# A hybrid encoder's attention and delta-rule scan in a fixed order of TensorE batches

## The chip, the cores and the metric

One core of a Trainium2 chip runs the whole program in one launch. The metric is the device time in microseconds (us), the median of several runs. One further execution was profiled; the rows below are from it.

## What is computed

Two layers on 512 tokens of width 1024, all in float32. Each layer is a feed-forward block (gate, up, down), a mixer and a second feed-forward block, each behind a root-mean-square norm and added to the stream. The mixer projects the stream to 16 heads of three kinds: 4 dense attention heads, 6 attention heads with a mask and a bias by distance, and 6 heads of a gated delta rule that is run over the tokens forwards and backwards. Their outputs go through one output projection.

The attention heads and the delta rule, cut to what matters here:

```python
s = q @ k.T * D ** -0.5 (+ bias);  p = softmax(s);  o = p @ v
...
T = triangular_solve(eye + M, eye)          # per chunk of 64 tokens, lower, unit diagonal
u, w = T @ vb, T @ (kb * exp(gc))
def step(state, xs):                        # 8 chunks, one behind the other
    v_new = u_i - w_i @ state
    o = (q_i * exp(g_i)) @ state + a_i @ v_new
    state = state * exp(g_last) + (k_i * exp(g_last - g_i)).T @ v_new
    return state, o
```

## The kernel before

Weights stream in by DMA and are split into two parts of 32 bits (`whi`, `wlo`), activations too (`xh`, `xl`), so that three matmuls stand for one in float32; the feed-forward blocks are made of these alone. In the mixer `project_c`, `project_z` and `project_groups` make the heads' inputs (`pc`, `pgr`), `delta_solve` inverts the chunks' triangular blocks, and `attention` runs the attention heads and, between them, the scan.

`delta_solve` inverts 32x32 diagonal blocks on VectorE (forward direction, d = 0) and GpSimd (d = 1), passes them through DRAM, and joins two blocks into one of 64 by two rows of 32x32 products (L649 into `pp1`, L658 into `pp2`), direction by direction and block by block: 12 products of one block, then 12 of the next. ScalarE copies `pp1` to `p1s` (L653) and `pp2` into `Y` (L662), 32 rows at a time.

`attention` has five tiles of two heads, and four query blocks (t) of 128 tokens each: 20 units. `scores` issues four matmuls into two `psc` (L868, L869), takes the row maximum on VectorE (L876, or L880 with the bias) and the exponential on ScalarE (L877, L882), and divides by the sum on GpSimd (L884). `weigh` transposes the probabilities on TensorE into `ppt` (L894), ScalarE copies them to `pth` (L896), and 8 matmuls of two halves add the values into `pav` (L900). `load(i)` transposes queries and keys into `pqk` (L813) and makes the split operands `qs`, `kh` on ScalarE (L820, L832) and `qs`, `kl` on VectorE (L821, L833); it is called at t = 2 of the tile ahead. `ppt` and `pqk` share two PSUM buffers, `psc` has two.

`delta_scan` is a generator with one step per chunk, which serves both directions (d) at once: products with the state `S` into `pkq` (L685), the right-hand side on VectorE (L688, L689, L691), the product with the inverse into `prr` (L697), `vn` (L700), the state's update into `pS` (L707, with GpSimd at L713 and VectorE at L715), and the output into `po` (L720, L727, L729, L731). Every matmul of float32 operands except a transpose is two records in a trace. `delta_finish` norms the output, transposes it into `pot` (L946) and multiplies by the gate; `project_out` is `pwo`.

A scheduler of the language sets each engine's order before the program runs, by priorities and an estimate of times. The order in which the code issues the work is only its starting point: it may put a unit's two transposes apart and other batches between them. `AHEAD = 1` puts `weigh` one unit behind `scores`, and `SCAN_AT` issues one whole scan step at every second unit:

```python
        for tile_ in range(5):
            for t in range(NT):
                pending.append(scores(tile_, t))
                if len(pending) > AHEAD:
                    weigh(*pending.pop(0))
                unit = 4 * tile_ + t
                for _ in range(SCAN_AT.count(unit)):
                    next(scan)
```

Of the kernel before, what the change touches and what calls it, by code (L numbers as in the profile page):

```python
# [29 lines left out]
SCAN_AT = (0, 2, 4, 6, 8, 10, 12, 14)  # L30
FINISH_AT = 15
LOAD_AT = 2
# [80 lines left out]
class Body:  # L113
# [205 lines left out]
    def mixer(self, n, l, sm, nxt):  # L319
# [4 lines left out]
        with scope("mix") as mp:  # L324
# [6 lines left out]
            with scope("qkv") as qkvp:  # L331
# [3 lines left out]
                with scope("scan") as sp, scope("scanp", space=PSUM) as m.ps:  # L335
# [10 lines left out]
                    with scope("outp", space=PSUM, **right) as pp:  # L346
                        if FINISH_AT >= 20:
                            m.delta_finish(sp)
                        m.project_out(pp, qkvp, nxt)


class Mixer:
# [244 lines left out]
    def delta_solve(self, pool):  # L597
# [42 lines left out]
        for d in range(2):  # L640
            y = self.Y[d]
            lo_a, lo_b = (0, 32) if d == 0 else (32, 0)
            rows = [(slice(64 * hf + lo_a, 64 * hf + lo_a + 32), slice(64 * hf + lo_b, 64 * hf + lo_b + 32)) for hf in range(2)]
            for tp in range(2):
                p1 = self.aux("pp1")
                for ra, rb in rows:
                    for q in range(12):
                        t, h = 2 * tp + q // 6, q % 6
                        nc.tensor.matmul(out=p1[rb, q * 32:q * 32 + 32], lhsT=y[ra, t, h, lo_b:lo_b + 32],  # L649
                                         rhs=X[ra, t * 6 + h], start=True, stop=True)  # L650
                ps = pool.tile([P, 384], F32, name="p1s")
                for ra, rb in rows:
                    nc.scalar.activation(out=ps[rb], in_=p1[rb, 0:384], func=AF.Copy)  # L653
                p2 = self.aux("pp2")
                for ra, rb in rows:
                    for q in range(12):
                        t, h = 2 * tp + q // 6, q % 6
                        nc.tensor.matmul(out=p2[ra, q * 32:q * 32 + 32], lhsT=ps[rb, q * 32:q * 32 + 32],  # L658
                                         rhs=y[rb, t, h, lo_b:lo_b + 32], start=True, stop=True)
                for ra, rb in rows:  # L660
                    dst = y[ra, 2 * tp:2 * tp + 2].rearrange("p t h i -> p (t h) i")[:, :, lo_b:lo_b + 32]
                    nc.scalar.activation(out=dst, in_=p2[ra, 0:384].rearrange("p (q i) -> p q i", i=32), func=AF.Copy)  # L662

    def delta_scan(self, sp):
# [8 lines left out]
        for s in range(8):  # L673
# [6 lines left out]
            if s > 0:  # L680
                pkq = two("pkq")
                for i in range(2):
                    for d, ch, t, r in dirs:
                        for pr in range(3):
                            nc.tensor.matmul(out=pkq[r, i, pr * P:pr * P + P], lhsT=self.kq[pr][:, i, ch], rhs=S[:, d, pr],  # L685
                                             start=True, stop=True)
# [5 lines left out]
            else:  # L692
                rhs = self.vs[:, 0]
            pr_ = self.aux("prr")
            for h in range(6):
                for d, ch, t, r in dirs:
                    nc.tensor.matmul(out=pr_[r, h * 64:h * 64 + 64], lhsT=self.Y[d][r, t, h],  # L697
                                     rhs=rhs[r, h * 64:h * 64 + 64], start=True, stop=True)
            vn = sp.tile([P, 384], F32, name="vn")
            nc.vector.tensor_tensor(out=hd(vn), in0=hd(pr_[:, 0:384]),  # L700
                                    in1=self.step[:, 0, s].unsqueeze(2).to_broadcast(sh), op=ALU.mult)
            if s < 7:
                pS = two("pS")
                for d, ch, t, r in dirs:
                    for h in range(6):
                        pr, par = divmod(h, 2)
                        nc.tensor.matmul(out=pS[64 * par:64 * par + 64, d, pr * 64:pr * 64 + 64],  # L707
                                         lhsT=self.kd[d][r, t, h * 64:h * 64 + 64], rhs=vn[r, h * 64:h * 64 + 64],
                                         start=True, stop=True)
# [8 lines left out]
            for h in range(6):  # L718
                for d, ch, t, r in dirs:
                    nc.tensor.matmul(out=po[r, h * 64:h * 64 + 64], lhsT=self.A[d][r, t, h],  # L720
                                     rhs=vn[r, h * 64:h * 64 + 64], start=True, stop=True)
# [75 lines left out]
    def attention(self, ap, pp, scan, sp):  # L797
# [3 lines left out]
        low, high = slice(0, 64), slice(64, 128)  # L801
        kept, pads = [], [ap.tile([P, 2, T], F32R, name=f"kl{i}") for i in range(2)]
# [7 lines left out]
        def turned(qkv, tl):  # L810
            p = pp.tile([P, T], F32, name="pqk", tag="t", bufs=2)
            for t in range(NT):
                nc.tensor.transpose(out=p[:, t * P:t * P + P], in_=qkv[:, t, tl * P:tl * P + P], identity=ident)  # L813
# [23 lines left out]
        ops = {}  # L837

        def load(i):
            if i < 2:  # L840
                if i == 0:
                    kv = keys(turned(self.qkv[0], 2), 1.0), self.qkv[0][:, :, 384:512]
                else:
                    kv = ops[0][1:]
                ops[i] = (queries(turned(self.qkv[0], i), 0.125), *kv)
            elif i < 5:
                g = self.qkv[i - 1]
                ops[i] = (queries(turned(g, 0), self.gq8), keys(turned(g, 1), self.nbk), g[:, :, 256:384])
# [3 lines left out]
        def scores(tile_, t):  # L852
            if t == 0:
                state["pv"] = pp.tile([P, T], F32, name="pav", tag="v")
# [7 lines left out]
            if t == LOAD_AT:  # L862
                load(tile_ + 1)
# [57 lines left out]
        for u in pending:  # L921
            weigh(*u)
# [136 lines left out]
```

## Time and profile before

| | us |
|---|---|
| median of 3 runs | 2238.77 |
| lowest, highest | 2235.66, 2243.84 |
| the profiled execution's time | 2234.65 |
| its span, first to last instruction | 2232.6 |
| TensorE busy in the span | 2179.1 (98%) |
| VectorE, ScalarE, GpSimd busy | 1138.8, 789.5, 483.7 |

The time of the profiled execution is its span and 2 us around it. Busy time of TensorE is the union of its records, whose ends are modelled: matmuls are pipelined, and a record is longer than the distance to the next. In a timeline, a row merges records of one line that follow each other; in square brackets stand the idle time before it and what ended that.

### The profile page before, as it was taken

How to read it: one execution, taken by the hardware profiler on the slowest of the kernel's cores; microseconds unless marked ns; L12 is line 12 of the kernel's file. 1: busy time of each engine (PE TensorE's matmuls, PEld its weight loads, DVE VectorE, ACT ScalarE, POOL GpSimd, SP SyncE). 2: the span in 40 equal slices, each digit the busy share in tenths (PEclk: the TensorE clock that was granted, in tenths of full speed). 3: DMA queues.
4: the chain of work that ended last, by engine and by line, in shares of the span. 5: the costliest groups of instructions: out<-in, count | busy, mean ns of one | idle time of the engine just before them, and what ended most of it. 6: DMA issues, size and time to landing. Idle time of an engine off the chain costs nothing.

```text
span 2232.6 us, 30294 instructions
## 1 busy us (share of the span) xinstructions
PE 2179.1 (98%) x12212; PEld 1745.9 (78%) x12212; DVE 1138.8 (51%) x1881; ACT 789.5 (35%) x1153; POOL 483.7 (22%) x490
## 2 busy tenths in 40 slices
PE   7999999998999999999999999999989999999999
PEld 5888887778777888888788888877787778888887
DVE  5333334688677533333443333347795765333333
ACT  4222223524565322222332222235345643222221
POOL 3101012217253210101121010123073531101010
PEclk9999999999999999999999999999999999999999
DMA  5433333232302333333233333332331033333333
GB/s 172 127 95 94 96 95 120 81 82 85 92 18 95 95 94 95 95 90 98 86 95 94 95 91 98 92 126 67 100 103 47 28 105 92 94 93 93 96 92 102
DMA packets 93076, 206.82 MB, mean 93 GB/s; under 512 B 38561, under 2 KB 39073, under 8 KB 92936
## 3 DMA queue, kind: packets, MB, share of 16 engines
q1 hardware_dynamic: 91168, 199.98, 30.0%
q10 hardware_dynamic: 1768, 4.91, 0.8%
q8 instruction: 96, 1.57, 0.3%
q14 instruction: 44, 0.36, 0.1%
HBM read 193.83 MB, written 14.18 MB: 93 GB/s over the span
## 4 chain that ended last, share of the span: by engine, by line
PE 88%; DVE 8%; ACT 2%; issue 1%; DMA 1%; POOL 0%; ACTq 0%; SPq 0%; DVEq 0%; POOLq 0%
PE pg L218 15%; PE pg L216 15%; PE pg L217 15%; PE pd L218 7%; PE pd L216 7%; PE pd L217 7%; PE pc L216 2%; PE pc L218 2%; PE pc L217 2%; PE pav L900 1%; PE ppt L894 1%; DVE wlo L211 1%; PE pwo L217 1%; PE pwo L216 1%; PE pwo L218 1%
## 5 line engine op out<-in xcount | busy, mean ns | idle before, releaser
L210 ACT ACTIVATE whi<-wraw 128x1024 fp32r<-128x1024 f32 (+3 forms) x344 | 351.4, 1022 | 1228.9 <-PE pg L217 651.7
L216 PE MATMUL pg<-xh,whi 128*128 128x512 f32 x1408 | 558.0, 397 | 8.5 <-ACT xh L236 8.3
L217 PE MATMUL pg<-xl,whi 128*128 128x512 f32 x1408 | 558.4, 397 | 2.3 <-DVE xl L237 2.2
L218 PE MATMUL pg<-xh,wlo 128*128 128x512 f32 x1408 | 557.8, 396 | 0.8 <-DVE wlo L211 0.8
L211 DVE TENSOR_TENSOR wlo<-wraw,whi 128x1024 fp32r<-128x1024 f32 (+3 forms) x344 | 408.4, 1187 | 89.0 <-ACT whi L210 83.5
L296 POOL TENSOR_TENSOR s<-s,rstd 128x512 f32<-128x512 f32 x88 | 152.7, 1737 | 1146.5 <-ACT s L295 1146.5
L216 PEld LDWEIGHTS pg<-xh,whi 128*128 128x128 f32 x1408 | 265.2, 188 | 73.2 <-ACT xh L236 8.3
L217 PEld LDWEIGHTS pg<-xl,whi 128*128 128x128 f32 x1408 | 265.0, 188 | 68.5 <-DVE xl L237 5.3
L218 PEld LDWEIGHTS pg<-xh,wlo 128*128 128x128 f32 x1408 | 265.1, 188 | 65.1 <-DVE wlo L211 1.9
L218 PE MATMUL pd<-hh,wlo 128*128 128x512 f32 x704 | 278.7, 396 | 0.9 <-DVE wlo L211 0.9
L216 PE MATMUL pd<-hh,whi 128*128 128x512 f32 x704 | 278.5, 396 | 0.0
L217 PE MATMUL pd<-hl,whi 128*128 128x512 f32 x704 | 278.4, 395 | 0.0
L310 DVE SCALAR_TENSOR_TENSOR x<-pd,x 128x512 f32<-128x512 f32 x96 | 66.3, 691 | 284.6 <-PE pd L218 284.6
L298 DVE TENSOR_TENSOR h<-pg,s 128x512 f32<-128x512 f32 x88 | 60.9, 691 | 287.8 <-PE pg L218 281.3
L294 DVE TENSOR_TENSOR s<-pg,rstd 128x512 f32<-128x512 f32 x88 | 60.6, 691 | 229.9 <-PE pg L218 229.7
L218 PEld LDWEIGHTS pd<-hh,wlo 128*128 128x128 f32 x704 | 132.3, 188 | 34.0 <-DVE wlo L211 2.2
L217 PEld LDWEIGHTS pd<-hl,whi 128*128 128x128 f32 x704 | 132.4, 188 | 31.9
L216 PEld LDWEIGHTS pd<-hh,whi 128*128 128x128 f32 x704 | 132.4, 188 | 31.7
L753 PE MATMUL pgr<-wlo,xh 128*128 128x384 f32 (+1 forms) x256 | 92.0, 360 | 11.2 <-DVE wlo L211 11.1
L884 POOL TENSOR_TENSOR prob<-prob,sm 128x512 f32<-128x512 f32 x80 | 84.6, 1066 | 78.5 <-DVE sm L883 63.5
L245 POOL TENSOR_TENSOR acc<-acc,sq 128x512 f32<-128x512 f32 x42 | 67.5, 1606 | 132.6 <-ACT sq L244 132.0
L754 PE MATMUL pgr<-whi,xl 128*128 128x384 f32 (+1 forms) x256 | 90.7, 354 | 0.0
(235 smaller groups left out, 2702.0 us busy)
## 6 DMA issues: line engine op xcount, KB each, us to landing
wraw<-in_gu_dram SPq DMA_DIRECT2D x176, 512.0 KB, 3.6
wraw<-in_wd_dram SPq DMA_DIRECT2D x64, 448.0 KB, 3.3
wraw<-in_wd_dram SPq DMA_DIRECT2D x32, 512.0 KB, 3.6
wraw<-in_w_c_dram SPq DMA_DIRECT2D x24, 512.0 KB, 3.6
wraw<-in_w_gb_dram SPq DMA_DIRECT2D x24, 384.0 KB, 3.1
wraw<-in_w_o_dram SPq DMA_DIRECT2D x14, 512.0 KB, 3.7
bias<-line SPq DMA_DIRECT2D x12, 448.0 KB, 5.0
saved<-x SPq DMA_DIRECT2D x16, 256.0 KB, 2.0
```

Of the source, the lines that this page charges most:

```text
L210: nc.scalar.activation(out=hi, in_=raw, func=AF.Copy)
L211: nc.vector.tensor_tensor(out=lo, in0=raw, in1=hi, op=ALU.subtract)
L216: nc.tensor.matmul(out=out, lhsT=w[0], rhs=x[0], start=first, stop=False)
L217: nc.tensor.matmul(out=out, lhsT=w[0], rhs=x[1], start=False, stop=False)
L218: nc.tensor.matmul(out=out, lhsT=w[1], rhs=x[0], start=False, stop=last)
L245: nc.gpsimd.tensor_tensor(out=n["acc"], in0=n["acc"], in1=sq, op=ALU.add)
L296: nc.gpsimd.tensor_tensor(out=s, in0=s, in1=n["rstd"], op=ALU.mult)
L298: nc.vector.tensor_tensor(out=h, in0=pp[1], in1=s, op=ALU.mult)
L310: nc.vector.scalar_tensor_tensor(out=self.x[dm], in0=p, scalar=0.5, in1=self.x[dm], op0=ALU.mult, op1=ALU.add)
L753: nc.tensor.matmul(out=o, lhsT=xh[:, tk], rhs=lo[:, wc], start=False, stop=False)
L754: nc.tensor.matmul(out=o, lhsT=xl[:, tk], rhs=hi[:, wc], start=False, stop=kk == KD - 1)
L884: nc.gpsimd.tensor_tensor(out=pb, in0=pb, in1=sm.to_broadcast([P, T]), op=ALU.mult)
```

## The change

It has four parts. The joined blocks of solve are computed in one function, `join_blocks`, which takes the four blocks (two directions, two halves) in turn, product by product, and copies `pp1` in one instruction; the copies of `pp2` are shared by ScalarE and VectorE. In the scan the two directions alternate in `pkq` and `pS`, and each step yields three times: behind the state products, behind `prr`, and at its end. `weigh` is split into `turn` (the transposes) and `weigh` (the sums), one and two units behind `scores`; `load` is split into `load_q` at t = 1 and `load_kv` at t = 3. And a context `batch` ties every batch's TensorE instructions behind the last marked one of the batch before: the scheduler can no longer mix them. The other engines' orders are still the scheduler's. The sums of the softmax (`sm`) also share one tile for two heads.

```diff
-SCAN_AT = (0, 2, 4, 6, 8, 10, 12, 14)
-FINISH_AT = 15
-LOAD_AT = 2
+SCAN_FROM = 0
...
+        self.join_blocks(pool, X)
+
+    def join_blocks(self, pool, X):
+        nc = self.nc
+        parts = []
+        for hf in range(2):
+            for d in range(2):
+                a, b = 64 * hf + 32 * d, 64 * hf + 32 * (1 - d)
+                parts.append((self.Y[d], slice(a, a + 32), slice(b, b + 32), slice(32 * (1 - d), 32 * (1 - d) + 32)))
+        turns = [(q, divmod(q, 6)) for q in range(12)]
+        for tp in range(2):
+            p1 = self.aux("pp1")
+            for q, (t, h) in turns:
+                t += 2 * tp
+                for y, ra, rb, cols in parts:
+                    nc.tensor.matmul(out=p1[rb, q * 32:q * 32 + 32], lhsT=y[ra, t, h, cols], rhs=X[ra, t * 6 + h],
+                                     start=True, stop=True)
+            ps = pool.tile([P, 384], F32, name="p1s", bufs=2)
+            nc.scalar.activation(out=ps, in_=p1[:, 0:384], func=AF.Copy)
...
+            for i, (y, ra, rb, cols) in enumerate(parts):
+                dst = y[ra, 2 * tp:2 * tp + 2].rearrange("p t h i -> p (t h) i")[:, :, cols]
+                src = p2[ra, 0:384].rearrange("p (q i) -> p q i", i=32)
+                if i % 2:
+                    nc.vector.tensor_copy(out=dst, in_=src)
+                else:
+                    nc.scalar.activation(out=dst, in_=src, func=AF.Copy)
...
                 for i in range(2):
-                    for d, ch, t, r in dirs:
-                        for pr in range(3):
...
+                    for pr in range(3):
+                        for d, ch, t, r in dirs:
...
+            if s > 0:
+                yield
             pr_ = self.aux("prr")
...
+            yield
             if s < 7:
                 pS = two("pS")
-                for d, ch, t, r in dirs:
-                    for h in range(6):
...
+                for h in range(6):
+                    pr, par = divmod(h, 2)
+                    for d, ch, t, r in dirs:
...
+        def mark(i):
+            here["next"] = i.ins
+            return i
+
+        @contextmanager
+        def batch():
+            last, here["next"] = here["last"], None
+            with self.tc.issue_after(last) if last is not None else nullcontext():
+                yield
+            here["last"] = here["next"] or last
...
-            if t == LOAD_AT:
-                load(tile_ + 1)
...
-        pending = []
-        load(0)
-        for tile_ in range(5):
-            for t in range(NT):
-                pending.append(scores(tile_, t))
-                if len(pending) > AHEAD:
-                    weigh(*pending.pop(0))
-                unit = 4 * tile_ + t
-                for _ in range(SCAN_AT.count(unit)):
-                    next(scan)
-                if unit == FINISH_AT:
-                    self.delta_finish(sp)
-        for u in pending:
-            weigh(*u)
...
+        for u in range(5 * NT + 2):
+            tile_, t = divmod(u, NT)
+            with batch():
+                if tile_ < 5:
+                    probs[u] = scores(tile_, t)
+            wide = SCAN_FROM <= u and (u - SCAN_FROM) % 2 == 0 and u < SCAN_FROM + 16
+            if wide:
+                with batch():
+                    if u > SCAN_FROM:
+                        advance()
+                with batch():
+                    weigh_at(u - 2)
+                with batch():
+                    turn_at(u - 1)
+                with batch():
+                    advance()
+            else:
+                with batch():
+                    turn_at(u - 1)
+                    if t == 1:
+                        load_q(tile_ + 1)
+                    if t == 3:
+                        load_kv(tile_ + 1)
+                with batch():
+                    weigh_at(u - 2)
+                if SCAN_FROM < u < SCAN_FROM + 16:
+                    with batch():
+                        advance()
+            if u == SCAN_FROM + 15:
+                next(scan, None)
+                self.delta_finish(sp)
```

TensorE's queue around the state products of one scan step (`pkq`, state products; `pav`, weighted sum; `ppt`, transposes; `psc`, scores; `prr`, product with the inverse). Before:

```order
L685 MATMUL pkq<-S,kq_3123 64x128
L685 MATMUL pkq<-S,kq_3124 64x128
L685 MATMUL pkq<-S,kq_3125 64x128
L900 MATMUL pav<-pth,qkv_4082 64x128 x7
L894 MATMUL ppt<-consts,prob 128x128 x4
L900 MATMUL pav<-pth,qkv_4082 64x128
L685 MATMUL pkq<-S,kq_3123 64x128
L685 MATMUL pkq<-S,kq_3124 64x128
L685 MATMUL pkq<-S,kq_3125 64x128
L868 MATMUL psc<-kh,qs 128x512
L869 MATMUL psc<-kl_4637,qs 128x512
```

and with the change:

```order
L690 MATMUL pkq<-S,kq_3124 64x128 x2
L690 MATMUL pkq<-S,kq_3125 64x128 x2
L690 MATMUL pkq<-S,kq_3123 64x128 x2
L690 MATMUL pkq<-S,kq_3124 64x128 x2
L690 MATMUL pkq<-S,kq_3125 64x128 x2
L930 MATMUL pav<-pth,qkv_4070 64x128 x8
L916 MATMUL ppt<-consts,prob 128x128 x8
```

A batch was cut where others fitted in: the sum of one unit stands in two pieces with transposes between them. Now the eight sums and eight transposes stand whole, with `prr` behind them and the next unit's scores behind that.

VectorE where the keys of a tile with a bias are loaded (`kl`), with the state's update (`S`) and the maxima (`ISA prob,nm`). Before:

```order
L833 SCALAR_TENSOR_TENSOR kl_4637<-pqk,nbk,kh 64x512
L883 RECIPROCAL sm<-sm 128x1
L700 TENSOR_TENSOR vn<-prr,step 128x384
L883 RECIPROCAL sm<-sm 128x1
L833 SCALAR_TENSOR_TENSOR kl_4637<-pqk,nbk,kh 64x512
L880 ISA prob,nm<-psc,bias 128x512
L880 ISA nm 128x1
L715 TENSOR_TENSOR S<-pS,S 64x6x64 x2
L883 RECIPROCAL sm<-sm 128x1
L727 TENSOR_TENSOR otok<-po,t_5173 64x384 x2
L880 ISA prob,nm<-psc,bias 128x512
```

and with the change:

```order
L899 TENSOR_REDUCE nm<-psc 128x1 x2
L906 RECIPROCAL sm<-sm 128x1 x2
L854 SCALAR_TENSOR_TENSOR kl_4625<-pqk,nbk,kh 64x512
L723 TENSOR_TENSOR S<-pS,S 64x6x64 x2
L735 TENSOR_TENSOR otok<-po,t_5111 64x384 x2
L903 ISA prob,nm<-psc,bias 128x512
L903 ISA nm 128x1
L854 SCALAR_TENSOR_TENSOR kl_4625<-pqk,nbk,kh 64x512
L906 RECIPROCAL sm<-sm 128x1
L903 ISA prob,nm<-psc,bias 128x512
L903 ISA nm 128x1
```

Both `kl` stood ahead of the state's update. Now the second one stands behind the update, both additions of `otok` and the first maximum of the next tile.

ScalarE at the same place (`kh`, keys; `pth`, copies of transposes; `prob,sm`, exponentials). Before:

```order
L877 ACTIVATE prob,sm<-psc,nm 128x512
L832 ACTIVATE kh<-pqk,nbk 64x512 x2
L896 ACTIVATE pth<-ppt 128x512
L877 ACTIVATE prob,sm<-psc,nm 128x512
L896 ACTIVATE pth<-ppt 128x512
L877 ACTIVATE prob,sm<-psc,nm 128x512
L832 ACTIVATE kh<-pqk,nbk 64x512 x2
L896 ACTIVATE pth<-ppt 128x512
```

and with the change:

```order
L918 ACTIVATE pth<-ppt 128x512 x2
L900 ACTIVATE prob,sm<-psc,nm 128x512
L918 ACTIVATE pth<-ppt 128x512 x2
L900 ACTIVATE prob,sm<-psc,nm 128x512
L853 ACTIVATE kh<-pqk,nbk 64x512 x4
L905 ACTIVATE prob,sm<-prob,nm 128x512 x2
```

Copies and exponentials took turns, with two `kh` at a time. Now an odd unit's first exponential stands ahead of both copies, and four `kh` stand together.

## Rows read from the trace of the kernel before

**Rows 1.** Timeline of TensorE, three scan starts; columns: start us, length us, engine, line, operation.
```profile
590.48 1.54 PE L697 MATMUL prr<-vs,Y 64*64 64x64 f32 x24 [1.06 <-ACT Y L662]
...
601.77 0.91 PE L697 MATMUL prr<-t,Y 64*64 64x64 f32 x24 [0.17 <-DVE t L689]
...
683.22 0.91 PE L697 MATMUL prr<-t,Y 64*64 64x64 f32 x24
```

**Rows 2.** Busy time by stretch: PE, PEld, DVE, ACT, POOL, then PEclk and DMA.
```profile
590.40:601.77 11.37, 10.38 (x109) 8.02 (x109) 7.58 (x15) 6.59 (x14) 2.61 (x4) 0.66 0.01 3
601.77:683.22 81.45, 78.16 (x1005) 61.41 (x1005) 59.53 (x140) 55.11 (x114) 47.32 (x48) 1.00 0.07 20
683.22:705.60 22.38, 21.60 (x214) 16.43 (x213) 19.55 (x59) 13.87 (x31) 11.64 (x11) 1.00 0.09 25
```

**Rows 3.** The last stretch again, records of line L868 alone (PE, PEld, clock, DMA).
```profile
683.22:705.60 22.38, 2.79 (x6) 1.14 (x6) 1.00 0.09 25
```

**Rows 4.** Timeline of TensorE, one batch of each kind in the stage.
```profile
653.43 1.77 PE L685 MATMUL pkq<-S,kq 128*64 128x128 f32 x24 [0.55 <-DVE S L715]
655.14 0.66 PE L894 MATMUL ppt<-consts,prob 128*128 128x128 f32 x4
...
656.50 0.48 PE L868 MATMUL psc<-kh,qs 128*128 128x512 f32 x1
...
657.60 1.09 PE L900 MATMUL pav<-pth,qkv 128*64 128x128 f32 x14
658.62 0.66 PE L894 MATMUL ppt<-consts,prob 128*128 128x128 f32 x4
659.20 0.92 PE L697 MATMUL prr<-t,Y 64*64 64x64 f32 x24
660.05 0.43 PE L900 MATMUL pav<-pth,qkv 128*64 128x128 f32 x2
...
663.00 0.62 PE L707 MATMUL pS<-vn,kd 64*64 64x64 f32 x19
...
664.36 0.66 PE L894 MATMUL ppt<-consts,prob 128*128 128x128 f32 x4
```

**Rows 5.** Timeline of TensorE, solve's block products.
```profile
576.64 1.49 PE L649 MATMUL pp<-X,Y 32*32 32x32 f32 x45
...
585.37 0.23 PE L649 MATMUL pp<-X,Y 32*32 32x32 f32 x2
...
585.46 0.19 PE L658 MATMUL pp<-Y,p1s 32*32 32x32 f32 x1
```

**Rows 6.** Groups by line and form, 560 to 591 us: busy us, mean ns, idle before.
```profile
L653 ACT ACTIVATE p1s<-pp 32x384 f32<-32x384 f32 x8 | 3.9, 482 | 1.1 <-PE pp L649 0.9
```

**Rows 7.** The same groups, 590 to 706 us, ScalarE.
```profile
L896 ACT ACTIVATE pth<-ppt 128x512 f32<-128x512 f32 x40 | 23.8, 594 | 19.4 <-PE ppt L894 19.2
...
L882 ACT ACTIVATE prob<-prob,nm 128x512 f32<-128x512 f32 x24 | 17.3, 720 | 6.9 <-DVE nm L880 6.2 <-DVE sm L883 0.4
...
L832 ACT ACTIVATE kh<-pqk,nbk 64x512 fp32r<-64x512 f32 x12 | 8.2, 681 | 1.0 <-PE pqk L813 0.8
```

**Rows 8.** The same groups, 590 to 706 us, VectorE.
```profile
L880 DVE CUSTOM_DVE_ANT_0 prob<-psc,bias 128x512 f32<-128x512 f32 x24 | 16.4, 684 | 4.3 <-PE ppt L894 2.6 <-PE psc L869 1.0 <-POOL prob L884 0.3
...
L715 DVE TENSOR_TENSOR S<-pS,S 64x384 f32<-64x384 f32 x14 | 7.8, 555 | 1.2 <-PE pS L707 0.5 <-POOL prob L884 0.5
...
L833 DVE SCALAR_TENSOR_TENSOR kl<-pqk,nbk,kh 64x512 fp32r<-64x512 f32 x6 | 4.5, 746 | 2.2 <-ACT kh L832 2.2
...
L727 DVE TENSOR_TENSOR otok<-po,t 64x384 f32<-64x384 f32 x6 | 3.3, 552 | 0.1
```

**Rows 9.** Timeline of TensorE, a wait for a transpose buffer.
```profile
631.65 0.63 PE L894 MATMUL ppt<-consts,prob 128*128 128x128 f32 x4 [0.84 <-ACT pth L896]
```

**Rows 10.** Groups by line and form, 590 to 706 us, GpSimd.
```profile
L884 POOL TENSOR_TENSOR prob<-prob,sm 128x512 f32<-128x512 f32 x40 | 42.3, 1066 | 39.4 <-DVE sm L883 31.9 <-PE pS L707 3.3 <-DVE ort L228 1.5
...
L713 POOL TENSOR_TENSOR S<-S,lstep 64x384 f32<-64x384 f32 x12 | 11.2, 934 | 0.8 <-PE pkq L685 0.3
```

More of the change, by code (lines that the diff above doesn't have):

```diff
@@ L1 @@
-from contextlib import ExitStack, nullcontext
+from contextlib import ExitStack, contextmanager, nullcontext
 import math
@@ L639, in delta_solve @@
                     dma.dma_start(out=X[32 * b:32 * b + 32], in_=s3[b].rearrange("s j i -> j s i"))
[L640 to L662, printed above, removed]
@@ new lines, in delta_solve @@
+        self.join_blocks(pool, X)
[16 more added lines that the diff above has]
+            nc.scalar.activation(out=ps, in_=p1[:, 0:384], func=AF.Copy)
+            p2 = self.aux("pp2")
+            for q, (t, h) in turns:
+                t += 2 * tp
+                for y, ra, rb, cols in parts:
+                    nc.tensor.matmul(out=p2[ra, q * 32:q * 32 + 32], lhsT=ps[rb, q * 32:q * 32 + 32],
+                                     rhs=y[rb, t, h, cols], start=True, stop=True)
+            for i, (y, ra, rb, cols) in enumerate(parts):
[5 more added lines that the diff above has]
+                    nc.scalar.activation(out=dst, in_=src, func=AF.Copy)
@@ L835, in keys, with load_q, load_kv @@
             return kh, kl
-        ops = {}
-        def load(i):
+        ops = [[None] * 3 for _ in range(6)]
+        def load_q(i):
             if i < 2:
[L841 to L845, printed above, removed]
+                ops[i][0] = queries(turned(self.qkv[0], i), 0.125)
+            elif i < 5:
+                ops[i][0] = queries(turned(self.qkv[i - 1], 0), self.gq8)
+        def load_kv(i):
+            if i == 0:
+                ops[0][1:] = keys(turned(self.qkv[0], 2), 1.0), self.qkv[0][:, :, 384:512]
+            elif i == 1:
+                ops[1][1:] = ops[0][1:]
             elif i < 5:
                 g = self.qkv[i - 1]
-                ops[i] = (queries(turned(g, 0), self.gq8), keys(turned(g, 1), self.nbk), g[:, :, 256:384])
+                ops[i][1:] = keys(turned(g, 1), self.nbk), g[:, :, 256:384]
         state = {}
@@ L868, in scores @@
                 nc.tensor.matmul(out=ps[par], lhsT=q[par][:, tk], rhs=kh[:, par], start=True, stop=False)
-                nc.tensor.matmul(out=ps[par], lhsT=q[par][:, tk], rhs=kl[:, par], start=False, stop=True)
+                mark(nc.tensor.matmul(out=ps[par], lhsT=q[par][:, tk], rhs=kl[:, par], start=False, stop=True))
             probs = []
+            sm = ap.tile([P, 2], F32, name="sm", bufs=2 * AHEAD + 2)
             for par in range(2):
@@ L897, in weigh @@
                 turns.append(full)
+            return turns
+        def weigh(turns, tile_, t):
+            tk = slice(t * P, t * P + P)
+            v = ops[tile_][2]
+            if t == 0:
+                state["pv"] = pp.tile([P, T], F32, name="pav", tag="v")
+            pv = state["pv"]
             for kt in range(NT):
                 for hb, full in zip((low, high), turns):
-                    nc.tensor.matmul(out=pv[hb, tk], lhsT=v[:, kt, hb], rhs=full[:, kt * P:kt * P + P],
-                                     start=kt == 0, stop=kt == NT - 1)
+                    mark(nc.tensor.matmul(out=pv[hb, tk], lhsT=v[:, kt, hb], rhs=full[:, kt * P:kt * P + P],
+                                          start=kt == 0, stop=kt == NT - 1))
             if t == NT - 1:
```

52 lines of the change are left out of this document (30 added, 22 removed).

## The prediction

> **What bounds the kernel now.** I read the busy times by stretch first. The two feed-forward blocks of each layer are untouched, so the question is the stage that the change rewrites: in layer 0 from the scan's first product at 590.48 us [rows 1] to the last weighted sum at about 705.6, 115 us; layer 1 has the same stage. TensorE is busy in 10.38 of 11.37, 78.16 of 81.45 and 21.60 of 22.38 us of its three stretches [rows 2]; VectorE has 59.53 of 81.45 in the middle and 19.55 of 22.38 in the last. So the stage hangs on TensorE's queue, and VectorE is close behind at the end. A busy TensorE is not TensorE at its rate, since a record contains its latency: cost is read from the start of one batch to the start of the next.
>
> I call one tile with one query block a unit (20 in the stage), and one chunk of both scan directions a step (8). From step 1 (601.77) to step 7 (683.22) [rows 1] are 81.45 us, 13.58 a step. In the last stretch three units' scores are left (6 records of the first score product, two a unit) [rows 3], so two units went into the first stretch, 15 into the middle one, 2.5 a step.
>
> **What the batches cost.** From start to start [rows 4]: four score matmuls 656.50 to 657.60, 1.10; four transposes with a change of shape behind them 658.62 to 659.20, 0.58, and without it 0.44, so eight are 1.02; a weighted sum 657.60 to 658.62, 1.02 (14 of its 16 records, so a little more); the state products pkq 653.43 to 655.14, 1.71; prr 659.20 to 660.05, 0.85; pS with po 663.00 to 664.36, 1.36. In the new order a step holds exactly two units: scores, state products, weighted sum, transposes, prr; then scores, transposes, weighted sum, pS, po. I take pkq at 1.50: no change of shape follows it, and two directions alternate. Sum: 2 x (1.07 + 1.02 + 1.02) + 1.50 + 0.85 + 1.36 = 9.93, and 10.37 with four transposes of a query or key load. That is the gain in sight: at 10.4 instead of 13.58 a step, though with two units instead of 2.5.
>
> **Start of the stage.** Part one is solve's products: 384 records a layer. In one chain of a single block they start 30 ns apart (45 in 1.49, of which 0.19 is the last one's own length); where two chains meet, eight start between 585.37 and 585.46, 12 ns [rows 5]. I take 12, so a batch of 96 is 1.15 instead of 2.9, and TensorE is spared 6.9 us in all. The copies out of PSUM go from 16 of 0.48 [rows 6] on ScalarE to two wide ones and eight that ScalarE and VectorE share, about 4.8 us of ScalarE. But the first batch now needs both directions' blocks, and its rows stand four matmuls behind where the second batch stood: I put it at 575.6. Then products, p1s, products, p1s, products, with 0.9 of transposes between, end at 582. Now the scores of unit 0 stand ahead of the scan's first product. They need four kh and two qs copies on ScalarE (0.68 each at most [rows 7]) behind a Y copy, and the kl and qs subtractions on VectorE (0.75 [rows 8]) behind its norm of the last projection group; I get 588.3 for the last, and prr at 589.3 instead of 590.48: **-1.2**. The lower clock is in both: PEclk averages 0.66 over the first stretch [rows 2], partly at 1.2 GHz. Step 0 itself gets longer, 13.1 against 11.3. In order: unit 1's scores need unit 0's exponentials, to 592.1; its query load waits for pth, which stands behind four exponentials, to 595; pS, po, unit 2's scores and VectorE's S then bring the state products to 598.3, and sum, transposes and right-hand side bring prr to 602.4. **+1.8**.
>
> The Trainium skill speaks against this part. "TensorE: Matmul & The Clock Gate", in "Wait — 56ns, not 53.3ns?", says that starts never come closer than about 25 ns, and "TensorEngine Tiling (Array Packing)", in "Restrictions and Gotchas", that row tiles cannot use one PSUM bank together, as the four blocks do. By 25 ns the 384 records would take an estimated 9.6 us, where 12 ns give 4.6. The eight starts in rows 5, in row strips that differ, contradict the first.
>
> **Steps 1 to 7.** Here the fixed order costs what it saves. TensorE can no longer pass a batch that isn't ready, and I find two that are late.
> (a) The loads of queries and keys moved into the odd units, right behind the transposes. There are two PSUM buffers for both, so the load waits until pth has copied the first. From the start of the unit's scores: maximum 0.75 to 1.44 (0.68 [rows 8]), exponential to 2.2 (0.72, and its sum is read behind it), pth to 2.8 (0.59 [rows 7]); the transposes end at 1.9, so the load starts at 2.9: 1.0 lost, in five of the six steps. Before, the same wait shows once as long, 0.84 at 631.65 [rows 9], since the order mixed other work in.
> (b) Keys are loaded in the last unit of a tile and needed in the next. ScalarE makes four kh from 3.9 to 6.7. VectorE's queue is kl, two S, two otok, maximum, kl: 5.4 + 0.75 + 2 x 0.56 + 2 x 0.55 + 0.68 + 0.75 = 9.8 [rows 8], and the second score pair needs that kl, where TensorE was free at 6.5: 3.4 lost with otok, 2.8 in the second half, where one addition stands for the two.
> So: one step of 9.93 + 0.3, three with a query load at 10.37 + 1.0 + 0.2 = 11.6, one with a key load at 10.37 + 1.0 + 3.4 + 0.4 = 15.2, and one at 10.37 + 1.0 + 2.8 + 0.8 = 15.0 (0.2 to 0.8 are for small waits on POOL, whose probabilities take 1.04 each and now queue behind S pairs of 0.93 each [rows 10]). Sum 75.2 against 81.45: **-6.2**.
>
> **The end.** At step 7, 15 units' scores are done instead of 17. Two units of 1.07 + 1.02 + 1.02 more make 22.4 into 28.6; VectorE has their maxima too. The transposes of otok stand ahead of unit 18's, but w_o's products still fill. I take 28: **+5.6**.
>
> **The sum.** -1.2 + 1.8 - 6.2 + 5.6 = 0.0 a layer. Against the profiled execution's 2234.65 that is 2234.6; it stands 0.2% under the median of the runs, so on their scale 2238. The unknown waits have both bounds: none in the steps, -13 a layer, and POOL late in each, +10.5; I take the walk between them, since it goes queue by queue, and keep both for the range.
>
> **The rivals.**
> *Waits covered, faster.* If the buffer and key waits fall into time when TensorE has queued work or the copies come earlier, steps run at TensorE's sum: 9.93 + 5 x 10.37 = 61.8 instead of 75.2, -13 a layer, 2212; with a shorter end 2206. For it: rows 2 show TensorE with work nearly throughout, and changes of shape become fewer. Against it: the new queue lets nothing pass. 0.32.
> *POOL, slower.* POOL has, in each step of the second half, four probabilities, two S and two otok, 4 x 1.04 + 4 x 0.95 = 8.0 us. The S pair waits for the state products and stands ahead of the even unit's probabilities, so these come up to 1.9 later; their transposes, due 1.10 + 1.50 + 1.02 + 1.02 + 0.85 + 1.03 = 6.5 us into the step, then wait, and with them everything. It decides where the second probability ends after 6.9, when the second four are due. At 1.5 a step in seven steps: +10.5 a layer, 2259. For it: before, POOL was busy 47.32 of 81.45 [rows 2], with the probabilities spread by the scheduler. Against it: with the products' results at 2.9, it is there at 2.9 + 2 x 0.93 + 2 x 1.04 = 6.8. 0.20.
> *Fours don't overlap.* The products stay at 30 ns; each of four batches is 1.7 longer, 6.9 in all, of which the waits for ScalarE take some 2.9: the scan starts 4 later, +4 a layer, 2246. The change would then not do what it says. The rule of 25 ns lies nearly there, with 1.25 a batch. 0.08.
>
> **How the numbers follow.** About 0.5%, 11 us, is what a measurement of this kernel tells from no change. The forecast, no change, has 0.40, with its own range from 2226 to 2250 (6 us a layer for the sizes of (a), (b) and the end). Faster: 0.32 and 0.02 of the forecast's edge; slower: 0.20, half of the 0.08 and 0.02; same takes the rest, 0.40. The range runs from the covered case's 2206 to 2262, just above POOL's.
>
> **What would show it.** Right: prr of steps 1 and 7 about 75 us apart; ppt of one unit together as eight; TensorE's idle before pqk ended by pth, about 1 us each, and before psc by kl, 2 to 4 us, twice; pp batches of 96 in about 1.2. The steps at 10.4 would prove the first rival, TensorE's idle before ppt ended by prob on POOL the second, pp at 25 to 32 ns the third. The forecast is wrong if the stage is over 6 us shorter or longer than 115.

## The result, and the profile after

The changed kernel takes 2262.22 us (median of 4 runs, 2258.58 to 2264.74) where the kernel before takes 2239.47 in the same comparison: ratio 1.0106, 95% interval 1.0088 to 1.0125. It is slower by 1.1%, and the median lies just above the range's end of 2262. The profiled execution took 2261.07, 26.4 more than the profiled one of before.

The head of the page of the changed kernel: span, busy times, and the DMA queue that brings TensorE's instructions.

```profile
span 2259.2 us, 30275 instructions
...
PE 2157.6 (96%) x12212; PEld 1729.1 (77%) x12212; DVE 1145.8 (51%) x1889; ACT 775.5 (34%) x1133; POOL 485.5 (21%) x490
...
q8 instruction: 96, 1.57, 0.3%
```

TensorE is busy 21 us less than before in a span that is 27 us longer. The work became shorter, and more than that was given back in waiting. The timeline of TensorE in layer 0 shows where: `prr` of steps 0, 1 and 7, and the last weighted sum.

```profile
593.74 1.55 PE L704 MATMUL prr<-vs,Y 64*64 64x64 f32 x24
...
606.74 0.92 PE L704 MATMUL prr<-t,Y 64*64 64x64 f32 x24 [0.62 <-DVE t L694]
...
686.96 0.92 PE L704 MATMUL prr<-t,Y 64*64 64x64 f32 x24 [0.52 <-DVE t L694]
...
720.55 1.09 PE L930 MATMUL pav<-pth,qkv 128*64 128x128 f32 x14
```

Against [rows 1] and the same points of layer 1, in us, each counted from the stage's first block product (569.0 before, 568.9 now; 1674.5 and 1688.6 in layer 1), the last sum by the start of its last record:

| stretch | forecast | layer 0 | layer 1 |
|---|---|---|---|
| first block product to `prr` of step 0 | -1.2 | 21.5 to 24.8: +3.3 | 22.2 to 24.0: +1.8 |
| step 0 | +1.8 | 11.3 to 13.0: +1.7 | 11.1 to 13.0: +1.9 |
| steps 1 to 7 | -6.2 | 81.4 to 80.2: -1.2 | 81.4 to 77.5: -3.9 |
| `prr` of step 7 to the last sum | +5.6 | 22.2 to 34.4: +12.2 | 22.2 to 34.5: +12.3 |
| sum | 0.0 | +16.0 | +12.1 |

The two layers make 28.1; what lies outside these stretches is some 1.7 shorter.

Busy time by stretch with the change: in layer 0 the start to step 1, steps 1 to 7 and the end, then steps 1 to 7 of layer 1. Columns: length; busy time of PE, PEld, DVE, ACT, POOL; PEclk; DMA share; GB/s.

```profile
568.90:606.70 37.80, 25.95 (x567) 20.54 (x566) 25.54 (x68) 19.42 (x41) 9.74 (x12) 0.82 0.31 68
606.70:687.00 80.30, 66.13 (x934) 53.98 (x935) 52.33 (x119) 41.69 (x91) 40.59 (x41) 0.96 0.06 20
687.00:721.40 34.40, 30.59 (x260) 23.41 (x260) 27.73 (x76) 21.27 (x46) 14.32 (x14) 0.90 0.05 13
1725.60:1803.20 77.60, 62.94 (x934) 50.95 (x935) 52.77 (x119) 41.67 (x91) 40.25 (x41) 1.00 0.06 21
```

Steps 1 to 7 read against [rows 2]: TensorE was busy 78.16 of 81.45 at full clock, idle 3.3. Now, with 12 units there instead of 15, it is busy 66.13 of 80.30, idle 14.2, and the clock is below 1.00. In layer 1, where the steps keep the full clock, it is busy 62.94 of 77.60, idle 14.7. Three narrower windows of layer 0, two of steps 1 to 7 and one of the end, show that the clock was at its lower level, 1.2 GHz, in whole stretches:

```profile
642.20:645.60 3.40, 3.40 (x36) 3.40 (x34) 1.75 (x5) 0.81 (x2) 1.56 (x2) 0.50 0.00 0
...
669.50:672.90 3.40, 3.40 (x27) 2.96 (x29) 1.02 (x4) 0.81 (x2) 1.71 (x2) 0.50 0.00 0
696.80:703.60 6.80, 6.30 (x30) 4.98 (x31) 4.43 (x12) 3.03 (x8) 2.77 (x3) 0.50 0.01 2
```

What runs at half clock takes nearly twice its time. Eight transposes in the end, at half clock and then at full clock, each with the weighted sum behind it:

```profile
697.89 1.91 PE L916 MATMUL ppt<-consts,prob 128*128 128x128 f32 x8
699.73 1.98 PE L930 MATMUL pav<-pth,qkv 128*64 128x128 f32 x16
...
703.51 1.10 PE L916 MATMUL ppt<-consts,prob 128*128 128x128 f32 x8
704.54 1.09 PE L930 MATMUL pav<-pth,qkv 128*64 128x128 f32 x16
```

From start to start the transposes take 1.84 and 1.03. By that ratio the 6.8 busy us at half clock in the steps cost some 3 (an estimate), and the 6.3 in the end 2.8. Layer 1 shows the first of these by measurement: the work of steps 1 to 7 at full clock is 62.9, 3.2 less than layer 0's. That of the end is then about 30.59 - 2.8 = 27.8.

The waits of TensorE from step 1 to step 7 of layer 0 (total us, times, longest):

```profile
PE pqk L834 <- ACT pth L918: 3.3, 4, 0.9
PE prr L704 <- DVE t L694: 2.7, 3, 1.6
PE psc L891 <- DVE kl L854: 2.7, 2, 1.5
PE psc L890 <- ACT kh L853: 1.8, 2, 0.9
PE prr L704 <- DVE sm L906: 1.4, 1, 1.4
PE pkq L690 <- DVE S L723: 1.3, 4, 0.4
PE ppt L916 <- POOL prob L907: 0.9, 2, 0.6
```

And TensorE's timeline in solve's products, where [rows 5] had chains and short mixed pieces; the first six products of the first batch stand 0.55 and more ahead of its first row:

```profile
575.89 0.97 PE L651 MATMUL pp<-X,Y 32*32 32x32 f32 x90
...
577.50 0.84 PE L659 MATMUL pp<-Y,p1s 32*32 32x32 f32 x75
579.72 0.35 PE L659 MATMUL pp<-Y,p1s 32*32 32x32 f32 x19 [1.38 <-issue]
...
579.92 1.02 PE L651 MATMUL pp<-X,Y 32*32 32x32 f32 x94
580.87 1.09 PE L834 MATMUL pqk<-consts,qkv 128*128 128x128 f32 x8
582.30 0.24 PE L659 MATMUL pp<-Y,p1s 32*32 32x32 f32 x3 [0.34 <-ACT p1s L654]
585.64 1.49 PE L659 MATMUL pp<-Y,p1s 32*32 32x32 f32 x93 [3.10 <-issue]
```

A batch of 96 takes about 1.0 (94 in 1.02, of which 0.2 is the last one's own length: 9 ns each), a little faster than forecast. But TensorE stands still twice in the middle of a batch, for "issue": nothing that the profile shows was missing. From the first stop to the second it started 19 + 4 + 94 + 8 + 3 = 128 matmuls (the 4 stand in rows left out), in layer 1 also 128 (there the stops are 0.91 and 2.66). The page's instruction queue moved 1.57 MB in 96 pieces, 16 KB each, for 24,424 matmuls and weight loads: about 256 instructions a piece, which are 128 matmuls with their loads. The trace also has the pieces' arrivals. The line of this queue in the DMA view of two single microseconds, 576 to 577 and 583 to 584:

```profile
q8 instruction: 1, 0.02, 7.7%
...
q8 instruction: 1, 0.02, 5.5%
```

The first piece starts at 576.9 and takes 1.2 us (7.7% of what 16 engines have in one), the second at 583.1 and takes 0.9. TensorE goes on at 579.72 and at 585.64, both times 1.6 behind the landing of a piece. So the theory: **TensorE used up a piece of its program faster than the next one came.**

### The profile page after: what moved, and what is told of

Read it like the earlier page. It is cut to its first block, busy times and chain, and to the rows that moved or that the text cites. A ratio compares the mean times of both kernels' runs of the same rounds, so it can differ in the third digit from the quotient of the medians.

```text
span 2259.2 us, 30275 instructions
## 1 busy us (share of the span) xinstructions
PE 2157.6 (96%) x12212; PEld 1729.1 (77%) x12212; DVE 1145.8 (51%) x1889; ACT 775.5 (34%) x1133; POOL 485.5 (21%) x490
## 3 DMA queue, kind: packets, MB, share of 16 engines
q8 instruction: 96, 1.57, 0.3%
## 4 chain that ended last, share of the span: by engine, by line
PE 83%; DVE 10%; ACT 3%; issue 2%; DMA 1%; POOL 0%; ACTq 0%; DVEq 0%; SPq 0%; POOLq 0%
PE pg L216 14%; PE pg L214 14%; PE pg L215 14%; PE pd L216 7%; PE pd L214 7%; PE pd L215 7%; PE pc L214 2%; PE pc L216 2%; PE pc L215 2%; PE pwo L214 1%; DVE wlo L209 1%; PE pwo L216 1%; PE pwo L215 1%; PE ppt L916 1%; PE pav L930 1%
## 5 line engine op out<-in xcount | busy, mean ns | idle before, releaser
L761 PE MATMUL pgr<-wlo,xh 128*128 128x384 f32 (+1 forms) x256 | 91.4, 357 | 12.2 <-DVE wlo L209 12.0
```

Of the source, the lines that this page charges most:

```text
L761: nc.tensor.matmul(out=o, lhsT=xh[:, tk], rhs=lo[:, wc], start=False, stop=False)
```

## The experiments

Three places lost time, and each had a theory: the block products outrun the instructions; the ties between batches turn every late operand into idle time, and the lower clock follows; the end has more units than before.

**Instructions, part one: the fours alone (e1).** The kernel before with `join_blocks` in place of its two rows of products, nothing else.

```diff
-        for d in range(2):
-            y = self.Y[d]
...
+        self.join_blocks(pool, X)
```

> The kernel before with solve's block products in fours and nothing else of the change. Theory (the batches of 96 outrun the supply of TensorE's instructions, which comes in blocks of 256 instructions, that is 128 matmuls with their weight loads): TensorE idles for 'issue' within these products, 1 to 3 us each time, with 128 products from one such idle to the next, and the product phase gains only what is left: the last product 2 to 4 us earlier a layer (589.2 before), the total 4 to 8 us lower, about 2234. Rival 1 (the idle comes from something in the changed scan or attention, not from the products): no idle for issue here, the last product at about 584, the total about 10 us lower. Rival 2 (the fours cost more than they save): slower than before.

2234.14 us, ratio 0.9986 (0.9975 to 0.9997). The stops are there without the changed scan:

```profile
577.71 0.35 PE L663 MATMUL pp<-Y,p1s 32*32 32x32 f32 x19 [1.16 <-issue]
...
583.91 1.50 PE L663 MATMUL pp<-Y,p1s 32*32 32x32 f32 x93 [3.18 <-issue]
```

They belong to the products, in the same two places of the batches. The fours still gain some 4 us in all (0.7 to 5.6 by the interval), though the scan's first product stands no earlier than before: 22.2 behind the first block product in layer 0, where 21.5 were measured.

**Part two: more products (e7).** The changed kernel with every first product issued twice.

```diff
-            for q, (t, h) in turns:
+            for q, (t, h) in turns * 2:
```

> The changed kernel with the first product of solve's blocks issued twice over (the same products into the same place): 192 more block products a layer, 384 more instructions of TensorE with their weight loads, no more copies. Theory (TensorE's instructions come in blocks of 256 and a block takes some 3.5 to 4 us to come, more than the 1.4 us in which 128 such products are issued): one or two more waits for issue a layer, 128 products apart, 3 to 6 us a layer: total 2268 to 2274. Rival (the waits for issue have another cause, and a product costs the 12 ns of its start): 192 times 12 ns, 2.3 us a layer, total 2264 to 2267, the waits for issue as many as before.

2276.39 us, ratio 1.0167 (1.0147 to 1.0188): 14.2 over the changed kernel, three times what 12 ns a product would give, and a little over the theory's own 12. TensorE's timeline, layer 0:

```profile
579.59 0.34 PE L651 MATMUL pp<-X,Y 32*32 32x32 f32 x17 [2.15 <-issue]
...
583.41 1.27 PE L651 MATMUL pp<-X,Y 32*32 32x32 f32 x128 [1.72 <-issue]
589.61 0.96 PE L651 MATMUL pp<-X,Y 32*32 32x32 f32 x53 [4.92 <-issue]
```

One row holds it whole: 128 products in 1.27, a stop ahead of them and a stop behind. The waits for issue in layer 0 are 8.8 in three instead of 4.5 in two, and each of the three ends 1.3 to 1.4 behind the landing of a piece. In layer 1 they are no more than before in number, 4.2 in two instead of 3.6, though the scan's first product comes 5.0 later there too; where the rest went is not shown. The page has 99 pieces instead of 96, for 768 instructions more: 256 a piece. The rival, a product that costs its 12 ns, falls.

**Part three: fours against rows, without ties (e11).** The ties taken out (as in e2 below) and solve's old rows put back.

> The changed kernel without ties and with solve's products block by block as before. Theory (in fours the products gain 2 to 4 us a layer in spite of the waits for instructions, as with the kernel before): no wait for issue over 1 us in the products, the last product 2 to 4 us later, total 2233 to 2238. Rival (the waits for issue give all of it back): 2227 to 2231.

2242.09 us, ratio 1.0016 (1.0002 to 1.0029), 12.6 over e2, more even than the theory had. The groups of the products by line, e11:

```profile
L654 PE MATMUL pp<-Y,p1s 32*32 32x32 f32 x192 | 7.7, 203 | 0.9 <-ACT p1s L649 0.9
...
L645 PE MATMUL pp<-X,Y 32*32 32x32 f32 x192 | 6.8, 192 | 0.6 <-DMA X<-s 0.6
```

and e2:

```profile
L659 PE MATMUL pp<-Y,p1s 32*32 32x32 f32 x192 | 3.0, 215 | 4.0 <-issue 3.1 <-ACT p1s L654 0.9
L651 PE MATMUL pp<-X,Y 32*32 32x32 f32 x192 | 2.5, 194 | 0.0
```

In rows the products keep TensorE busy 14.5 us and never wait for issue; in fours 5.5, and 3.1 of waiting (in layer 1 5.4 and 4.8). That leaves 5.9 and 4.3 for the fours, 10.2 of the 12.6. Where it shows differs: from the first block product to the last sum e2 is 6.2 shorter than e11 in layer 0, but 0.3 in layer 1. So the fours are worth having, and the supply of instructions takes a third of what they save in layer 0 and half in layer 1; the exact size is not settled.

**The ties (e2).**

```diff
-            last, here["next"] = here["last"], None
-            with self.tc.issue_after(last) if last is not None else nullcontext():
-                yield
-            here["last"] = here["next"] or last
+            yield
```

> The changed kernel with the ties between the batches taken out: the scheduler may mix TensorE's batches again; solve in fours, three scan parts and the sums two units behind stay. Theory (the fixed order pays in waits for the buffer, the keys and the lower clock that follows them): the waits of TensorE for pth before pqk (3.3 us in steps 1 to 7) and for kh and kl (4.5) mostly go, the end of the stage is shorter than 34 us, total 2240 to 2250. Rival (the fixed order itself saves changes of shape and the loss lies in what it issues, not in the ties): total within 5 us of 2262 or above it.

2229.50 us, ratio 0.9955 (0.9938 to 0.9973): 32.7 under the changed kernel, better than the theory's 2240, and 0.45% under the kernel before. By stretch, steps 1 to 7 and the end:

```profile
607.10:676.90 69.80, 69.23 (x978) 54.38 (x978) 54.78 (x128) 47.66 (x100) 43.16 (x43) 1.00 0.08 23
676.90:702.20 25.30, 22.76 (x204) 16.22 (x202) 22.50 (x65) 15.74 (x34) 11.43 (x10) 1.00 0.07 22
```

TensorE's work in the steps is longer than with the ties, 69.2 against 62.9, in part because more stands there (978 records against 934) and in part, as far as can be told, because batches are cut again; but it is idle for 0.6 instead of 14.2 and keeps its clock. At an equal time a record the ties save some 3 us of work there (an estimate) and pay 14 of idle time and, in layer 0, 3 of clock.

**One step of freedom (e5).** Each batch is tied to the last but one.

```diff
-            last, here["next"] = here["last"], None
+            last, here["next"] = here["prev"], None
...
+                here["prev"], here["last"] = here["last"], here["next"]
```

> The changed kernel with each batch tied to the last batch but one instead of the last: two neighbouring batches may be mixed or exchanged. Theory (TensorE stands idle because nothing may pass a batch that is not ready; before, the scheduler let the neighbours pass): the idle time of TensorE in steps 1 to 7 falls from 14 us to 3 to 8, its work stays shorter than before (under 70 us where 78 were), total 2235 to 2248. Rival (what is late is late whatever stands next to it; only the scheduler's long-range moves, by several batches, cover it): idle stays over 10 us, total 2255 to 2263.

2232.69 us, ratio 0.9966 (0.9955 to 0.9978): 29.5 of the 32.7 come back, a little more than the theory had. Steps 1 to 7:

```profile
606.20:674.20 68.00, 65.23 (x953) 51.52 (x952) 53.10 (x124) 43.06 (x91) 41.16 (x42) 1.00 0.08 23
```

Idle 2.8, work 65.2. What was late was late by little, and a neighbour was enough to cover it. The rival, that only long-range moves help, falls.

**Single waits under the full ties (e3, e9).** e3 loads the next tile's keys one unit earlier:

```diff
-                    if t == 3:
-                        load_kv(tile_ + 1)
...
+                if t == 2:
+                    with batch():
+                        load_kv(tile_ + 1)
```

> The changed kernel with the keys of the next tile loaded one unit earlier (at t = 2, behind prr, instead of t = 3). Theory (the scores of a tile's first unit wait for kh and kl, and TensorE's clock falls to half behind these waits): the waits for kh and kl, 4.5 us in steps 1 to 7 and 2.2 at the end, go, and so do the half-clock stretches behind them (two of 3.4 us and one of 6.8 in layer 0, one of 6.8 in layer 1): 8 to 13 us less a layer, total 2238 to 2246. Rival (another wait of the same size takes their place, since ScalarE and VectorE have the same work ahead of the same scores): total 2255 to 2263.

2255.34 us, ratio 1.0071 (1.0053 to 1.0089), 6.9 less, at the lower edge of the rival's range. The waits for kh and kl are gone from the steps and so are the half-clock stretches there, but others came or grew (from step 1 to step 7 of layer 0):

```profile
PE prr L704 <- DVE t L694: 5.1, 5, 1.6
PE ppt L916 <- ACT pth L918: 2.6, 2, 1.5
PE pqk L834 <- ACT pth L918: 2.2, 3, 0.9
```

Idle time of TensorE in the steps went from 14.2 to 13.0 in layer 0 and from 14.7 to 12.7 in layer 1, though 4.5 of waits for keys are gone in each. Under full ties a wait that is cured is for more than half replaced. Layer 0's steps are 5.5 shorter, some 3 of it the half clock; layer 1's, which had none, 3.1.

e9 fills the waits for keys instead, with 8 matmuls whose result is overwritten, in the first unit of tiles 2 to 4:

```diff
             for par in range(2):
+                if par and t == 0 and tile_ >= 2:
+                    past = ops[tile_ - 1][1][0]
+                    for i in range(8):
+                        mark(nc.tensor.matmul(out=ps[1], lhsT=q[0][:, tk], rhs=past[:, i % 2], start=True, stop=True))
```

> The changed kernel with 8 matmuls more (1.9 us at 0.23 each) ahead of the second head's scores in the first unit of tiles 2, 3 and 4, where TensorE waits for kh and kl; their result is overwritten by the scores. Theory (the wait itself is short, but TensorE's clock falls to half behind it, and that costs as much again): the waits there shrink by most of 1.9 us each, the half-clock stretches at 642, 669 and 697 us and their like in layer 1 go, and with them 6 us in layer 0 and 3 in layer 1: total 2252 to 2257, though there is more work. Rival 1 (the other engines' chains set the pace, and a slower TensorE is hidden behind them): the stretches go, total 2260 to 2264. Rival 2 (the fall has another cause than the wait): the stretches stay, total 2262 or more.

2263.24 us, ratio 1.0108 (1.0089 to 1.0126), no change. Busy time by stretch, around the first of these waits, and in all of steps 1 to 7:

```profile
638.50:646.50 8.00, 7.16 (x80) 5.67 (x78) 6.83 (x15) 3.98 (x8) 2.73 (x3) 1.00 0.00 0
...
607.60:684.30 76.70, 65.78 (x949) 53.77 (x949) 53.31 (x119) 41.44 (x90) 40.13 (x41) 1.00 0.06 21
```

In the steps of layer 0 the theory holds: with the wait filled the clock stays up, and the steps take 76.7 instead of 80.3, 3.6 less where half clock had cost some 3. The other runs agree. The steps of e3, which also lack these waits, are at 1.00 in both layers; those of e4, e6 and e7, which keep the ties and the waits, are at 0.94 to 0.96 in all six. It was the wait that let the clock fall. As a whole the theory missed, and the total lies in the first rival's range, whether for its reason or not: at the end the wait for kl grew to 2.3 and a half-clock stretch of 3.4 stayed, layer 1 had no such stretch in its steps to lose, and 24 matmuls a layer are 5.5 us of work.

**The end (e6).** The ties stay through unit 14 and are dropped behind it.

```diff
+            with self.tc.issue_after(last) if last is not None and here["unit"] < 15 else nullcontext():
```

> The changed kernel with the ties kept through unit 14 and dropped from unit 15 on, so that only the last units and the end of the scan may be mixed. Theory (of the 33 us that the ties cost, some 8 to 10 a layer are lost in the end, where the last five units stand in a chain): from step 7's prr to the last weighted sum 25 to 28 us instead of 34.4, total 2242 to 2248. Rival (the end is long because two units more are left there, each with its maxima, exponentials and probabilities): still over 31 us, total 2256 to 2262.

2261.65 us, ratio 1.0100 (1.0076 to 1.0124): the rival's total. The end by stretch:

```profile
693.50:725.30 31.80, 28.75 (x257) 21.01 (x256) 25.36 (x75) 20.83 (x45) 14.60 (x14) 1.00 0.06 18
```

It is 2.6 shorter (1.2 in layer 1), no more: 112 records of weighted sums, seven units' worth, still lie behind step 7's `prr`, as with the full ties, where before had 96 and e2's layer 0 82. The end is long for what is left to do. Of the 3.8 us that the two layers' ends lost, the total shows 0.6, which its interval does not tell from either.

**The start of the scan (e4, e12) and the units around it (e8, e10).** e4 moves `prr` of step 0 ahead of unit 0's scores, under full ties.

> The changed kernel with the scan's first product (prr of step 0) ahead of unit 0's scores instead of behind them. Theory (behind the last block product, prr waits 5.5 us longer than before because scores that wait for qs stand ahead of it on TensorE): prr 4 to 5 us earlier in both layers, and step 1's prr 2 to 4 earlier since the scan's chain runs while the scores wait; total 2254 to 2258. Rival (TensorE's work is what counts, and the scores are only moved): prr earlier, step 1's prr within 1 us of 606.7, total 2261 to 2264.

2262.28 us, ratio 1.0108 (1.0087 to 1.0129): the rival.

```profile
587.52 0.47 PE L704 MATMUL prr<-vs,Y 64*64 64x64 f32 x2
591.28 1.54 PE L704 MATMUL prr<-vs,Y 64*64 64x64 f32 x22 [3.28 <-DVE Y L665]
...
607.55 0.91 PE L704 MATMUL prr<-t,Y 64*64 64x64 f32 x24 [0.62 <-DVE t L694]
```

`prr` now waits for a copy of Y, and step 1's is no earlier: in between stand the same scores, transposes and a query load.

e12 does the same without ties and for pS and po too:

> The changed kernel without the ties, and in its first two units the scan's parts (prr, then pS and po) are issued ahead of the scores instead of behind them, as in the kernel before. Theory (without ties step 1's prr stands at 607.1 where 601.8 was before, because at the start the scores of three units and their copies are put ahead of a scan whose chain then runs late; TensorE has idle and half-clock time there to lose): step 1's prr 3 to 6 us earlier, total 2219 to 2227. Rival (TensorE has work nearly throughout behind step 1, so that what is done earlier for the scan is done later for the units): step 1's prr earlier, the total within 3 us of the 2229.5 without ties alone.

2231.11 us, ratio 0.9964 (0.9954 to 0.9975), the rival again; step 1's `prr` did not even come earlier (608.1), since the scheduler put the scores ahead of it all the same.

e8 starts the scan two units later, without ties (`SCAN_FROM = 2`):

> The changed kernel without the ties, and with the scan started two units later, so that two units fewer are left behind it. Theory (without ties TensorE has work nearly throughout, and units that are moved from the end to the start move their work with them): the end shorter by 4 to 6 us a layer, the start longer by as much, total 2226 to 2234. Rival (at the start TensorE waits for copies and runs at half clock, so that two units there cost nothing): total 2215 to 2224.

2244.72 us, ratio 1.0018 (1.0000 to 1.0036): both missed, 15 slower than e2. The end is shorter, 19.5 in layer 0, but the way to step 1's `prr` is 41.7 where e2 has 37.9, and steps 1 to 7 take 74.5 instead of 69.8. Why the steps grew is open.

e10 joins e5 and e3:

> Ties to the last batch but one, and the keys loaded one unit earlier. Theory (with neighbours free to pass, the keys' waits are mostly gone already: 1.1 us for kh in layer 0's steps): total 2228 to 2233, no more than 4 under the loose ties alone. Rival (earlier keys are worth what they gave under the full ties, 7 us): total 2223 to 2227.

2237.62 us, ratio 0.9990 (0.9980 to 1.0001), 5 slower than e5 alone: both missed. With loose ties the steps are no shorter for it (68.6), and the end is 2 longer. So the earlier keys were a cure for the ties, and none for the kernel.

## Why the prediction was wrong

**The work was right.** The sum of batch costs gave 61.8 us for steps 1 to 7, and 62.9 were measured at full clock (layer 1); for the end 28.6, and about 27.8. Products in fours start about 9 ns apart, where 12 was taken. Step 0 was forecast at +1.8 and came at +1.7 and +1.9.

**The start failed in the term of the block products.** "products, p1s, products, p1s, products, with 0.9 of transposes between, end at 582" priced each batch at its own pace. It ended at 587. The 4.5 us (3.6 in layer 1) of waits for issue were in no term; with them `prr` is at 593.7 where 589.3 was forecast. The rival "fours don't overlap" had 4 us for a wrong reason: they overlap so well that their instructions can't follow. That the supply is the cause is what e1, e7 and the landings of the pieces show; what sets how fast a piece comes was not tested.

**Steps 1 to 7: the idle time was right in sum, partly by luck, and the clock was missing.** 75.2 less 61.8 are 13.4 of waits; 14.2 were measured, 14.7 in layer 1. (a), the buffer ([rows 9] of before), is 0.8 to 0.9 four times, where 1.0 five times was forecast. (b), the keys, is 2.5 and 2.0 where 3.4 and 2.8 stood. What these fall short is made up by `prr`, which waits for VectorE, 4.1 in all; the walk did not have that: with pkq, one sum and one set of transposes close together, the right-hand side stands behind two maxima. What remains is the clock. The forecast spoke of the lower clock at the start alone; the waits for keys brought it into the steps, some 3 in layer 0 (none in layer 1, where the same waits did not lower it). e9 shows that it came from the wait. So the steps gained 1.2 and 3.9 where 6.2 was forecast.

**The end failed as a term.** "I take 28" was the work, with "w_o's products still fill". It took 34.4: 3.8 idle (the last tile's keys 2.2 of it) and some 2.8 of half clock behind them stand beside the work, +12.2 instead of +5.6. That two units more lie there was forecast, and e6 shows that what lies there, and not the ties inside the end, makes most of its length.

**The rivals.** "Waits covered" named what decides: e2 and e5, where TensorE may pass a late batch, take steps of 68 to 71, though not the 61.8 of that rival. "POOL, slower" had 2259, near the result, but not for its reason: TensorE waited 0.9 for probabilities from step 1 to step 7 of layer 0, where 1.5 a step was priced. A total that comes out right does not prove its mechanism.

## What to carry to other kernels

A fixed order of batches is only as fast as its latest operand at each place; price the work and the waits apart, and then the clock that a wait lets fall, which in layer 0 cost nearly as much again as the waits for keys. Leaving each batch one neighbour to pass gave back nine tenths of the loss, so tie loosely. The version without ties took the least, 2229.5 us, 0.45% under the kernel before (e12, 2231.1, cannot be told from it). Without the products in fours nothing of that gain is left (e11), and the fours alone gave 0.14% (e1); why the two give more together is not shown.

## What the runs showed of the hardware that was not expected

- **Instructions have a supply rate.** Products 9 ns apart run for 128 matmuls and then stop, for 0.2 to 4.9 us, until 1.3 to 1.6 behind the landing of a piece (the changed kernel and e7, both layers); at 30 ns apart (e11) they don't stop. The Trainium skill, "Runtime: NRT & Kernel Launch", in "Instruction fetch mechanics", says that instructions come in blocks of 256 and that crossing a block is mostly hidden. The trace agrees with the block and disagrees with the rest: 4.5 us were exposed in one layer.
- **A short wait can halve TensorE's clock.** Two waits of 0.91 and 1.55 us ahead of scores were followed by 3.4 us at 1.2 GHz in layer 0, and like ones in layer 1 were not; in e4, e6 and e7 the steps of both layers show it (0.94 to 0.96).
- **A VectorE operation on 12 numbers a row took 1.04 us** in the end, where its like takes 0.17, beside a GpSimd multiplication over just that time. VectorE, and then GpSimd, in the timeline of the changed kernel:

```profile
704.47 0.17 DVE L225 TENSOR_TENSOR ort<-orq 128x12 f32<-128x12 f32 x1
...
705.08 1.04 DVE L225 TENSOR_TENSOR ort<-orq 128x12 f32<-128x12 f32 x1
...
705.06 1.04 POOL L907 TENSOR_TENSOR prob<-prob,sm 128x512 f32<-128x512 f32 x1 [3.66 <-DVE orq L227]
```

The chain of the output's norm goes through such operations. Three of them in layer 0's end (0.90, 1.04 and 0.70 us) end together with the GpSimd multiplication beside them, and ahead of the longest wait of `prr` (1.59) an addition of 0.54 elsewhere took 1.39 beside two of them. That the two engines hinder each other fits this, and was not tested.
